# Differential-attention scores as row-split float products: two maps of a head in partitions 0 to 63 and 64 to 127

## The chip, the cores and the metric

The kernel runs on one core of one Trainium2 chip. The metric is the device time of one execution in microseconds (us), lower is better. The time before is the median of three runs.

## The reference, cut to what matters

The reference is a two-layer block over 1024 latent tokens and 256 context tokens, width 1024. Each layer has a combined input projection, three mixers (differential attention with 4 heads, a state-space scan, a Fourier mixer), an output projection and a squared-ReLU MLP. The change touches the attention scores:

```python
def one_block(qblk):                       # 128 queries
    s = jnp.einsum('bqhmd,bkhmd->bmhqk', qblk, k).astype(jnp.float32) * scale
    p = jax.nn.softmax(s, axis=-1)
    w = p[:, 0] - lam * p[:, 1]            # two maps m of each head h
    return jnp.einsum('bhqk,bkhd->bqhd', w.astype(v.dtype), v)
```

A head has two maps, each with its own query and key of 64 elements; the values of a head have 128. Queries of latent tokens see all 1280 keys; in the first layer the context's queries see the 256 context keys.

## The kernel before, in words

Products with float32 accuracy are made of float32r products, a float32r operand taking one pass of TensorE: an operand is split into a high part (its float32r rounding) and a low part (the rest). `stack` (L538 to 546) transposes the normalized queries and keys of a tile of 128 tokens and writes both parts to DRAM: `QD[t, e]` and `KD[h, e]`, e = 0 the high part and e = 1 the low one, with the two maps of a head in rows 0 to 63 and 64 to 127.

`attention` (from L615) runs once per layer, and a *unit* is one head of one tile of 128 queries. Layer 0 has 8 latent tiles and 2 context tiles (32 full units and 8 of context alone), layer 1 has 8 latent tiles (32 full units).

- `load_k` (L620 to 624) loads a head's keys: for each map a tile `ST[h][m]` whose rows 0 to 63 hold the high part and rows 64 to 127 the low part, in four transfers of 64 rows. `load_q` (L626 to 633) loads a tile's queries: `QS[e]` holds part e twice, in the lower and in the upper 64 rows, for both maps. That takes four transfers, and each byte of `QD` is loaded twice. All go through SP's queue.
- `scores` (L635 to 660): a product of 128 rows with `QS[0]` is then high times (high + low), and one with `QS[1]` is low times (high + low). So a map's scores of 512 keys are two products (`product`, L638 to 640). First come the context keys of both maps into `C`, one PSUM bank (four products of 256 columns) with one maximum over both (L647). Then, map by map, the latent keys go into `S`, two banks (four products of 512 columns), with their maximum (L654), the smaller of the negated maxima (L655), and the exponential on ScalarE (L656), which also sums; L657 does the same for `C`.
- `combine` (L662 to 672): one row sum over the other, and map 0 minus lambda times map 1 on VectorE (L668; in layer 1 the last 512 keys on GpSimd, L670 and L671).
- `values` (L674 to 696): ten transposes (L682), copies to SBUF on ScalarE (L683), ten float32 products with the values (L686, two instructions each), the scaling by the row sum (L688).
- The loop at the end takes `combine` and `values` of the unit three before around the `scores` of the new one. `yield` gives three of four units a piece of other work: the state space's gate (`glu`, L1037 to 1050, which reads `HD`) and, in layer 0, the modulation's products (`mod_pe`, L414, 512 columns in float32).

PSUM in this stage has eight banks: pool `s` with two buffers of [128, 1024] (two banks each) and pool `b` with four banks for `C`, the transposes and the value products. A buffer of a pool is given to the next tile when everything that reads the old one is done.

The order of instructions on each engine is fixed when the program is built: a list scheduler takes, of what its own timeline holds ready, what comes first in the program. So instructions of one unit may be put between those of another. `keep_in_program_order(ins)` ties an instruction behind the one traced before it on its engine.

At the start of the stage SP's queue carries, besides queries and keys, the last state-space transfers: `pa_t<-PD` (L945), the stores `HD<-kv_t` (L1017) and the load `kv_t<-HD` (L1037), which L1046 reads.

## Time and profile before

| what | value |
|---|---|
| median of 3 runs | 3081.3 us (3078.29 to 3085.9) |
| the profiled execution's own time | 3084.44 us |
| its span, first to last instruction | 3082.5 us |
| mean granted TensorE clock | 0.983 of full speed |
| busy share: TensorE (PE), weight loads (PEld), VectorE (DVE), ScalarE (ACT), GpSimd (POOL) | 96%, 78%, 64%, 35%, 20% |

A line of the profile names engine, source line and operands; `L640` is a line of the kernel before. The duration of a TensorE product reaches to the modelled end of its result, so consecutive products overlap in the rows: the distance from start to start (*pitch* below) tells what one costs, and the duration of a merged group is (count - 1) pitches and one duration. PEld rows are the weight loads of the products. In the view of busy times by stretch the columns are: stretch (us from the start), its length, busy us of PE, PEld, DVE, ACT and POOL with their counts of instructions (or of the chosen line's engine alone), granted clock, share of the DMA engines, GB/s.

### The profile page before, as it was taken

The page shows a single profiled execution, that of the slowest core. Times are in us where ns is not written, and L with a number is a line of the kernel's source. Part 1 is how long each engine was busy: PE and PEld are TensorE (multiplying, and loading weights), DVE is VectorE, ACT ScalarE, POOL GpSimd, SP SyncE. Part 2 cuts the span into 40 slices and gives each one's busy share as a digit, 9 for nine tenths or more (in the row PEclk, how much of TensorE's full clock was granted, in tenths as well). Part 3 has the DMA queues.
Part 4 walks back from the last instruction along what each step waited for, and adds up shares of the span by engine and source line. Part 5 has one row for each costly group of instructions (what it writes and reads, how often), then busy time and mean ns, then how long its engine had stood idle before and what let it go on. Part 6 is the DMA issues. An engine that isn't in the chain of part 4 may idle for free.

```text
span 3082.5 us, 41061 instructions
## 1 busy us (share of the span) xinstructions
PE 2950.3 (96%) x15309; PEld 2417.6 (78%) x15309; DVE 1972.9 (64%) x3527; ACT 1077.3 (35%) x2387; POOL 620.5 (20%) x534
## 2 busy tenths in 40 slices
PE   5889989999999999999999999989999999999999
PEld 2667767668888888888888777768889888888887
DVE  7786757666577777676545556959866555455444
ACT  5323436656331121121222243437863222211222
POOL 2563420000100000000276123526631000000000
PEclk8999989999999999999999999999999999999999
DMA  7445573435113232231222044571241111111111
GB/s 244 160 150 165 171 172 113 134 110 154 52 49 103 64 98 84 83 95 43 72 74 89 28 148 141 154 182 52 66 139 44 52 45 55 48 48 41 55 48 65
DMA packets 280851, 299.93 MB, mean 97 GB/s; under 512 B 47158, under 2 KB 191948, under 8 KB 280652
## 3 DMA queue, kind: packets, MB, share of 16 engines
q1 hardware_dynamic: 280652, 297.31, 32.1%
q8 instruction: 120, 1.97, 0.3%
q14 instruction: 79, 0.65, 0.1%
HBM read 229.31 MB, written 67.93 MB: 96 GB/s over the span
## 4 chain that ended last, share of the span: by engine, by line
PE 78%; DVE 9%; DMA 5%; ACT 2%; issue 2%; POOL 1%; SPq 0%; DVEq 0%; POOLq 0%; ACTq 0%
PE b_t L1202 26%; PE b_t L1225 25%; PE b_t L1169 6%; PE b_t L575 4%; PE b_t L686 3%; PE s_t L640 3%; PE b_t L414 2%; PE b_t L602 2%; PE b_t L682 1%; DVE mx L654 1%; DMA s_t<-KD 1%; ACT s_t L656 1%; DMA qs_t<-QD 1%; DMA r_t<-in_w_in_dram 1%; DVE w_t L160 1%
## 5 line engine op out<-in xcount | busy, mean ns | idle before, releaser
L1225 PE MATMUL b_t<-hid_t,w_t 128*128 128x512 f32 (+1 forms) x3840 | 809.3, 370 | 0.0
L1202 PE MATMUL b_t<-s_t,w_t 128*128 128x512 f32 (+1 forms) x3840 | 800.4, 369 | 0.0
L1225 PEld LDWEIGHTS b_t<-hid_t,w_t 128*128 128x128 f32 x3840 | 669.9, 189 | 121.3 <-issue 1.4
L1202 PEld LDWEIGHTS b_t<-s_t,w_t 128*128 128x128 f32 x3840 | 669.0, 189 | 121.3 <-issue 1.1
L1227 DVE SCALAR_TENSOR_TENSOR kv_t<-b_t,mod,kv_t 128x512 f32<-128x512 f32 (+1 forms) x640 | 439.8, 695 | 238.6 <-PE b_t L1225 238.0
L159 ACT CAST w_t<-r_t 128x512 fp32r<-128x512 f32 x336 | 195.1, 619 | 796.1 <-PE b_t L1225 528.7
L575 PE MATMUL b_t<-w_t,s_t 128*128 128x512 f32 (+1 forms) x1392 | 357.7, 411 | 10.0 <-DVE kv_t L1227 3.8
L160 DVE TENSOR_TENSOR w_t<-r_t,w_t 128x512 fp32r<-128x512 f32 x320 | 223.7, 726 | 214.1 <-ACT w_t L159 213.5
L575 PEld LDWEIGHTS b_t<-w_t,s_t 128*128 128x128 f32 x1392 | 266.5, 198 | 72.6 <-issue 6.6
L133 POOL TENSOR_TENSOR sm<-sm,mhalf 128x8 f32<-128x8 f32 (+3 forms) x66 | 106.7, 1616 | 543.2 <-DVE sm L693 232.1
L1206 DVE TENSOR_TENSOR t_t<-b_t,t_t 128x512 f32<-128x512 f32 x160 | 101.2, 633 | 139.4 <-ACT t_t L1205 139.3
L881 POOL TENSOR_TENSOR bg_t<-pt_t,bw_t 128x256 f32<-128x256 f32 x56 | 43.8, 782 | 695.4 <-DMA bw_t<-BD 668.7
L686 PE MATMUL b_t<-kv_t,kv_t 128*128 128x128 f32 x1312 | 177.7, 280 | 3.4 <-ACT kv_t L683 3.3
L686 PEld LDWEIGHTS b_t<-kv_t,kv_t 128*128 128x128 f32 x1312 | 163.8, 193 | 16.7 <-ACT kv_t L683 7.2
L654 DVE TENSOR_REDUCE mx<-s_t 128x1 f32<-128x1024 f32 x128 | 155.2, 1219 | 22.5 <-PE s_t L640 21.8
L159 ACT CAST hid_t<-t_t 128x512 fp32r<-128x512 f32 x160 | 92.5, 578 | 207.0 <-DVE t_t L1206 206.9
L1205 ACT ACTIVATE t_t<-b_t 128x512 f32<-128x512 f32 x160 | 88.2, 552 | 207.3 <-PE b_t L1202 207.2
L656 ACT ACTIVATE s_t<-s_t,mx 128x1024 f32<-128x1024 f32 x128 | 143.6, 1122 | 25.1 <-DVE mx L655 19.4
L160 DVE TENSOR_TENSOR hid_t<-t_t,hid_t 128x512 fp32r<-128x512 f32 x160 | 105.8, 662 | 66.2 <-ACT hid_t L159 66.2
L375 DVE SCALAR_TENSOR_TENSOR ac_t<-bg_t,vc,ac_t 128x512 f32<-128x512 f32 x168 | 118.8, 745 | 32.9 <-DMA bg_t<-in_w_mod_dram 32.5
L640 PE MATMUL s_t<-s_t,qs_t 128*128 128x512 f32 x448 | 128.8, 412 | 9.0 <-ACT s_t L656 6.0
L602 PE MATMUL b_t<-w_t,s_t 128*128 128x512 f32 x480 | 116.5, 396 | 2.5 <-DVE w_t L160 1.4
(329 smaller groups left out, 3581.5 us busy)
## 6 DMA issues: line engine op xcount, KB each, us to landing
r_t<-in_w_ff_dram SPq DMA_DIRECT2D x256, 256.0 KB
bg_t<-in_w_mod_dram SPq DMA_DIRECT2D x96, 256.0 KB
r_t<-in_w_in_dram SPq DMA_DIRECT2D x64, 256.0 KB
qs_t<-QD SPq DMA_DIRECT2D x64, 256.0 KB
XD<-kv_t SPq DMA_DIRECT2D x16, 640.0 KB
KD<-t_t SPq DMA_DIRECT2D x40, 256.0 KB
s_t<-KD SPq DMA_DIRECT2D x32, 320.0 KB
QD<-t_t SPq DMA_DIRECT2D x36, 256.0 KB
```

Source lines behind the costliest of these rows:

```text
L159: self.nc.scalar.copy(h, raw)
L160: (eng or self.nc.vector).tensor_tensor(l, raw, h, ALU.subtract)
L575: nc.tensor.matmul(p[:, :cols], a[:, ts], W[k][:, b, :cols], start=(n == 0), stop=(n == 23))
L602: nc.tensor.matmul(p, a[:, ts], W[k][:, b], start=(n == 0), stop=(n == 11))
L640: nc.tensor.matmul(dst, QS[e][:, m, h], ST[h][m][:, a:b], start=(e == 0), stop=(e == 1))
L654: nc.vector.tensor_reduce(mx[:, m, 1:2], S, AX.X, ALU.max, negate=True)
L656: nc.scalar.activation(PR[m][:, 0:SEQ], S, AF.Exp, bias=mx[:, m, 0:1], accum_out=sm[:, m, 1:2])
L686: nc.tensor.matmul(o, WT[:, kt * 128:(kt + 1) * 128], V[kt // 5][:, kt % 5, h * 128:(h + 1) * 128], start=(c == 0), stop=(c == len(ks) - 1))
L1169: nc.tensor.matmul(p[:, :w], W[c][a][:, k], b[k][:, s:s + w], start=(n == 0), stop=(n == 23))
L1202: nc.tensor.matmul(p[:, :w], W[a][:, k], b[k][:, s:s + w], start=(q == 0), stop=(q == 23))
L1225: nc.tensor.matmul(p[:, :w], W[a][:, cs], hid[b][:, s:s + w], start=(q == 0), stop=(q == n - 1))
L1227: nc.vector.scalar_tensor_tensor(xs, p[:, :w], self.mod[l][:, 40 + c, g // 2:g // 2 + 1], xs, ALU.mult, ALU.add)
```

## The change

Each part of `QD` and `KD` is loaded once as it lies in DRAM: both maps of a part in one tile of 128 rows, two transfers instead of four for a tile of queries and for a head's keys. A map's scores are three products over 64 rows (high·high, low·high, high·low) instead of two over 128 rows. Map 0 uses rows 0 to 63 of TensorE and map 1 rows 64 to 127; the products of the two are interleaved by a count of columns and tied in that order. The order for a full unit is, with (map: keys a, product q): C0 q0, S1a q0, C0 q1, S1a q1, C0 q2, S0a q0, S1a q2, S0a q1, S1b q0, S0a q2, S1b q1, S0b q0, S1b q2, S0b q1, S0b q2, then C1 q0 to q2 (a and b are the first and second 512 latent keys). `S` of both maps is one tile of four banks, with one buffer. The maximum of `C` is taken map by map.

```diff
         def load_k(h):
             ST.append([self.s5([128, TOK], F32R) for _ in range(2)])
-            for m in range(2):
-                for e in range(2):
-                    nc.sync.dma_start(ST[h][m][e * 64:e * 64 + 64].bitcast(F32), self.KD[h, e, m * 64:m * 64 + 64])
+            for e in range(2):
+                nc.sync.dma_start(ST[h][e].bitcast(F32), self.KD[h, e])
 
         def load_q(t, pool='qs'):
-            QS = [self.tl(pool, [128, 2, 4, 128], F32R) for _ in range(2)]
+            QS = [self.tl(pool, [128, 4, 128], F32R) for _ in range(2)]
             for e in range(2):
-                src = self.QD[t, e].rearrange('(m d) c -> d m c', m=2)
-                for r in range(2):
-                    dst = QS[e][r * 64:r * 64 + 64].rearrange('p m h c -> p m (h c)')
-                    nc.sync.dma_start(dst.bitcast(F32), src)
+                nc.sync.dma_start(QS[e].bitcast(F32), self.QD[t, e].rearrange('p (h c) -> p h c', h=NH))
             return QS
 
         def scores(h, t, QS, n):
             full = t < 8
-
-            def product(dst, m, a, b):
-                for e in range(2):
-                    nc.tensor.matmul(dst, QS[e][:, m, h], ST[h][m][:, a:b], start=(e == 0), stop=(e == 1))
-
             C = self.pb((128, 2, CTX))
-            for m in range(2):
-                product(C[:, m], m, SEQ, TOK)
+            if full:
+                S = self.tl('s', [128, 2, SEQ])
+                S = [S[:, m] for m in range(2)]
...
-            nc.vector.tensor_reduce(mx[:, :, 0], C, AX.X, ALU.max, negate=True)
             PR = [E[m][n % 4] for m in range(2)]
-            for m in range(2):
-                if full:
-                    S = self.tl('s', [128, SEQ])
-                    for a in (0, 512):
-                        product(S[:, a:a + 512], m, a, a + 512)
-                    nc.vector.tensor_reduce(mx[:, m, 1:2], S, AX.X, ALU.max, negate=True)
-                    nc.vector.tensor_tensor(mx[:, m, 0:1], mx[:, m, 0:1], mx[:, m, 1:2], ALU.min)
-                    nc.scalar.activation(PR[m][:, 0:SEQ], S, AF.Exp, bias=mx[:, m, 0:1], accum_out=sm[:, m, 1:2])
+
+            def product(m, a, q):
+                e, f = ((0, 0), (1, 0), (0, 1))[q]
+                r = slice(m * 64, m * 64 + 64)
+                b = min(a + 512, SEQ) if a < SEQ else TOK
+                dst = S[m][:, a:b] if a < SEQ else C[:, m]
+                return nc.tensor.matmul(dst, QS[e][r, h], ST[h][f][r, a:b], start=(q == 0), stop=(q == 2))
+
+            rows = [[(0, SEQ, q) for q in range(3)], []]
+            if full:
+                rows[0] += [(0, a, q) for a in (0, 512) for q in range(3)]
+                rows[1] += [(1, a, q) for a in (0, 512) for q in range(3)]
+            rows[1] += [(1, SEQ, q) for q in range(3)]
+            at = [0, 0]
+            while rows[0] or rows[1]:
+                m = 0 if rows[0] and (rows[1][0][1] == SEQ or at[0] <= at[1]) else 1
+                x = rows[m].pop(0)
+                at[m] += 288 if x[1] == SEQ else 544
+                ins = product(*x)
+                if full and x[:2] != (1, SEQ) and x != (0, SEQ, 0):
+                    self.tc.keep_in_program_order(ins)
+                if x == (0, SEQ, 2):
+                    nc.vector.tensor_reduce(mx[:, 0, 0:1], C[:, 0], AX.X, ALU.max, negate=True)
+            if full:
+                nc.vector.tensor_reduce(mx[:, 1, 1:2], S[1], AX.X, ALU.max, negate=True)
+            nc.vector.tensor_reduce(mx[:, 1, 0:1], C[:, 1], AX.X, ALU.max, negate=True)
+            for m in ((1, 0) if full else ()):
+                if m == 0:
+                    nc.vector.tensor_reduce(mx[:, m, 1:2], S[m], AX.X, ALU.max, negate=True)
+                nc.vector.tensor_tensor(mx[:, m, 0:1], mx[:, m, 0:1], mx[:, m, 1:2], ALU.min)
+                nc.scalar.activation(PR[m][:, 0:SEQ], S[m], AF.Exp, bias=mx[:, m, 0:1], accum_out=sm[:, m, 1:2])
+            for m in (1, 0):
                 nc.scalar.activation(PR[m][:, SEQ:TOK], C[:, m], AF.Exp, bias=mx[:, m, 0:1], accum_out=sm[:, m, 0:1])
...
-            with self.scope(psum={'s': 2, 'b': 4}, qs=4, ax=3, ot=2, jk=1, bg=1, mw=1):
+            with self.scope(psum={'s': 1, 'b': 4}, qs=4, ax=3, ot=2, jk=1, bg=1, mw=1):
```

## Rows read from the trace of the kernel before

**Rows 1.** Page, part 1: busy us, share of the span, instructions.
```profile
PE 2950.3 (96%) x15309; PEld 2417.6 (78%) x15309; DVE 1972.9 (64%) x3527; ACT 1077.3 (35%) x2387; POOL 620.5 (20%) x534
```

**Rows 2.** Busy times by stretch: the attention of layer 0, then of layer 1.
```profile
440.00:735.00 295.00, 277.87 (x1667) 201.73 (x1668) 203.73 (x407) 193.77 (x516) 19.71 (x18) 1.00 0.41 118
2080.00:2276.00 196.00, 186.21 (x1339) 169.09 (x1338) 167.48 (x326) 159.70 (x422) 126.07 (x78) 0.98 0.22 59
```

**Rows 3.** The same view of L659 alone (DVE, one per full unit).
```profile
446.00:724.00 278.00, 6.16 (x31) 1.00 0.39 116
2100.50:2265.00 164.50, 9.75 (x27) 0.99 0.22 55
```

**Rows 4.** Timeline, PE, layer 0: start, us, engine, line, operation, out<-in, shapes, count.
```profile
450.23 0.63 PE L640 MATMUL b_t<-s_t,w_t 128*128 128x256 f32 x4
...
500.61 1.09 PE L640 MATMUL s_t<-s_t,qs_t 128*128 128x512 f32 x4
501.53 1.25 PE L682 MATMUL b_t<-idn,s_t 128*128 128x128 f32 x10
502.62 1.56 PE L686 MATMUL b_t<-kv_t,kv_t 128*128 128x128 f32 x12
```

**Rows 5.** Timeline, PE, 158 us: products of 64 rows between products of 128.
```profile
157.76 1.09 PE L575 MATMUL b_t<-w_t,s_t 128*128 128x512 f32 x4
158.78 0.27 PE L897 MATMUL f_t<-bg_t,bw_t 64*16 64x112 f32 x1
158.79 0.27 PE L899 MATMUL f_t<-bg_t,bw_t 64*16 64x112 f32 x1
158.89 0.26 PE L897 MATMUL f_t<-bg_t,bw_t 64*16 64x112 f32 x1
...
159.08 1.20 PE L575 MATMUL b_t<-w_t,s_t 128*128 128x512 f32 x4
```

**Rows 6.** Timeline, PEld, 529 us: weight loads of 128 columns.
```profile
529.06 0.57 PEld L421 LDWEIGHTS b_t<-idn,bg_t 2*128 2x128 f32 x8
```

**Rows 7.** Groups of DVE, 2100 to 2265 us: count, busy us, mean ns, idle before.
```profile
L654 DVE TENSOR_REDUCE mx<-s_t 128x1 f32<-128x1024 f32 x54 | 65.8, 1219 | 7.2 <-PE s_t L640 7.1
...
L647 DVE TENSOR_REDUCE mx<-b_t 128x2 f32<-128x512 f32 x26 | 17.9, 687 | 7.1 <-PE b_t L640 6.4
...
L655 DVE TENSOR_TENSOR mx<-mx 128x1 f32<-128x1 f32 x54 | 8.2, 155 | 0.3
```

**Rows 8.** Chain of waits, 2099 us: start, us, an exponential with its sum.
```profile
2099.25 1.21 ACT s_t L656 x2
```

**Rows 9.** Waits of PE, 400 to 735 us: us in total, times, longest.
```profile
PE f_t L970 <- DMA pa_t<-PD: 6.7, 1, 6.7
PE s_t L640 <- ACT s_t L656: 3.1, 10, 0.8
...
PE b_t L1046 <- DMA kv_t<-HD: 2.5, 1, 2.5
```

**Rows 10.** Waits of PE, 2045 to 2276 us.
```profile
PE b_t L1046 <- DMA kv_t<-HD: 7.1, 1, 7.1
PE s_t L640 <- ACT s_t L656: 5.5, 7, 1.4
```

**Rows 11.** Busy times by stretch: start of layer 1's attention; columns as in rows 2.
```profile
2025.00:2045.00 20.00, 20.00 (x100) 16.64 (x99) 13.02 (x29) 4.84 (x14) 8.08 (x6) 1.00 1.04 234
2045.00:2065.00 20.00, 17.66 (x82) 13.79 (x81) 9.90 (x18) 1.08 (x3) 1.22 (x1) 1.00 1.01 221
```

**Rows 12.** Timeline of SP's queue: start, us of issuing, transfers.
```profile
442.32 3.70 SPq L1017 DMA_DIRECT2D HD<-kv_t  x8
...
2048.70 4.69 SPq L632 DMA_DIRECT2D qs_t<-QD  x4
2054.31 8.71 SPq L1017 DMA_DIRECT2D HD<-kv_t  x8
```

**Rows 13.** Page, part 6: transfers by line, KB each.
```profile
qs_t<-QD SPq DMA_DIRECT2D x64, 256.0 KB
```

## The prediction

> **What bounds the kernel now.** The page comes first: PE is busy 96% of the span [rows 1]. The change touches two stretches only, so the busy times by stretch come next: the attention of layer 0 takes 295 us, that of layer 1 196 us, and in the second PE (95%), DVE (85%) and ACT (81%) are all close to full [rows 2]. The reader should see there that a faster PE soon meets DVE and ACT. L659 runs once per full unit and so gives the period: 278 us for 31 units, 8.97 us in layer 0 (other work and context units included), and 164.5 us for 27, 6.09 us in layer 1 [rows 3].
>
> What PE needs for a unit follows from pitches, (duration of a merged row - duration of one) / (count - 1), with one product at 0.39, 0.28, 0.27 and 0.28 us for the four forms: 0.233 us for the 512 columns of L640, 0.117 for its 256 columns, 0.109 for L682 and 0.116 for L686 [rows 4]. A unit's scores are 8 x 0.233 + 4 x 0.117 = 2.33 us, its transposes 10 x 0.109 = 1.09, its value products 20 x 0.116 = 2.32, a quarter of the tile's last four transposes 0.11: 5.85 of layer 1's 6.09 us. PE sets the pace there, with 0.2 us of waiting.
>
> The waits of PE show what else is on the path: 6.7 and 2.5 us for PD and HD in layer 0, 7.1 us for HD in layer 1, and 3.1 and 5.5 us in which scores wait until the exponential has freed `S` [rows 9, 10].
>
> **The scores on PE.** Does 64 + 64 rows run two products at once? The nearest rows say so: L897 (rows 0 to 63) starts at 158.78 and L899 (rows 64 to 127) at 158.79, and the next pair 0.11 later [rows 5]. Each stream then has 6 x 0.233 + 3 x 0.117 = 1.75 us, and the last product of `C` hangs over by 0.12: 1.87 us for 2.33, a gain of 0.46 us.
>
> Going in and out costs some of it. The fourth L575 starts at 157.76 + 3 x 0.233 = 158.46 and the next product was due at 158.69; L897 comes 0.09 later. The way back: a pitch of 0.11 after 158.89 would be 159.00, and L575 comes at 159.08, 0.08 later. The four L575 behind it take 1.20 instead of 1.09 us, so a load that no product covers costs 0.11 [rows 5]; with 128 columns I charge it at the entry too. In and out: 0.09 + 0.11 + 0.08 + 0.11 = 0.39 us. So a unit whose 18 products stand together gains 0.07 us, 64 units 5 us (**-5**). The page TensorEngine Tiling (Array Packing) of the Trainium skill, section Key Properties, says that a change of the tiling mode drains TensorE, which speaks against this change; the trace agrees, 0.09 and 0.08 us late. The page gives no price; without the drain and its bare loads the sum would stand at 64 x 0.46 = 29 us of gain here, with the rows' price it is 5.
>
> Weight loads rise from 12 to 18. Eight loads of 128 columns take 0.57 us, 0.14 of which is one load's own, a pitch of 0.06 [rows 6]: 1.1 us beside 1.87 of products, hidden. The Trainium skill, page TensorE: Matmul & The Clock Gate, section LDWEIGHTS, gives columns / 1.2 as nanoseconds, 107 for one; one after the other, 18 would take 1.92 us, 0.05 over the products, and by that rule the sum would be 3 us longer. The rows' 0.06 stands in the sum.
>
> Two things are not tied. The first product of `C` may be put early, between transposes or value products of another unit; it then costs a second way in and out, 0.39 us, in layer 0, where other work fills PE: 0 to 12 us for 32 units. No row here says how often; every unit would have to be hit for the upper end, so I take a quarter (**+3**). And the eight context units have three products per map, one map after the other with one overlap, 5 x 0.117 for 4 x 0.117, plus 0.39: 8 x 0.5 (**+4**).
>
> **The ring of `S`.** Before, each map had its own buffer. Now both lie in one tile with one buffer, and the next unit's scores wait for both exponentials. From the first product into `S`: bare load 0.11, last product of map 1 at 5 x 0.233, its end 0.39 later: 1.67 us. Then on DVE the maximum of map 1 1.22, of `C` of map 1 about 0.42 (an estimate: L647's 0.69 for 512 columns less half of L654's 1.22 - 0.69), the smaller 0.155, map 0's maximum 1.22 and the smaller 0.155 [rows 7], then map 0's exponential with its sum 1.21 [rows 8]: 6.05 us until `S` is free. Map 1's exponential runs beside map 0's maximum. Before, one map needed 3 x 0.233 + 0.39 + 1.22 + 0.155 + 1.21 = 3.7 of 6.09 us, so the buffers had slack; now there is none, and any work of DVE that gets between is added. DVE has 167.48 / 32 = 5.2 us per unit [rows 2], 1.8 of it outside this chain, with the first `C` maximum 2.2; free for that are 6.05 + 1.67 - 4.84 = 2.9 us from map 0's smaller (at 4.84) to the next unit's first maximum. It fits with little room, so I take 6.15 us for layer 1: 32 x 0.06 (**+2**). Bounds: the ring hidden and PE's 5.78 setting the pace, 32 x -0.31 = -10; half a microsecond of DVE work in the ring of each unit, 6.55, 32 x 0.46 = +15. In layer 0 the mean of 8.97 us hides it; the fourth of the units without other work may lose 0 to 0.5 us, 0 to 4 us (**+1**). `C` now has two maxima, 0.84 for 0.69 us, within the 2.2.
>
> **The transfers.** A tile of queries was four transfers of 256 KB [rows 13], 1.05 MB, and is now half; the keys' bytes stay. From 2025 to 2065 us all DMA engines are full at 221 to 234 GB/s [rows 11], so half a tile is 2.3 us. In layer 1 SP's queue takes 4.7 us to issue tile 1's queries and then 8.7 us for the eight HD stores that took 3.7 in layer 0 [rows 12]: 1.3 MB less ahead of the HD load is 5.7 us, of which the stores can give back 8.7 - 3.7 = 5.0 of PE's 7.1 us wait. In layer 0 half a tile lies ahead of PD (2.3 of 6.7 us), and HD's 2.5 us may go. That is 9.8 us at most and nothing at least, if what the gate needs on ACT or DVE is late next; I take **-7**. Eight key transfers instead of sixteen also shorten SP's queue, counted in these bounds. The exponentials' change of order is free: ACT is 81% busy and they start when DVE lets them.
>
> **Sum.** -5 + 4 + 3 + 2 + 1 - 7 = -2 us against the profiled execution's 3084.4 us (span 3082.5 and 1.9 around it), which lies 3.1 us above the median: 3079 us against 3081.3. 0.3%, 9.2 us, is about what a measurement of this kernel can tell from no change.
>
> **The rivals.** *The ring takes more than it looks (slower).* Place: DVE's order between the two maxima of a unit. Price: layer 1 +15 and layer 0 +4, with the other terms -3 (layer 0's half of the -5) + 4 + 3 - 7: +16, 3097 us. For it: no slack in 6.05, and DVE's idle time before L654 and L647 is only 0.5 us a unit [rows 7]. Against: 2.9 us are open for 2.2. It decides the sign from a period of 6.44 us, where 32 x 0.35 = 11 us outweighs the other terms (-2) by 9.
> *The ring hides and the queues clear (faster).* Layer 1 -10, layer 0 -3 + 4, transfers -10: -19, 3062 us. For it: the 5.5 us of waits for `S` [rows 10] and full DMA engines. Against: the same 6.05.
> *The products don't run side by side*, so that the change doesn't do what it says: 12 x 0.233 + 6 x 0.117 + 0.39 - 2.33 = 1.56 us more in 64 units, 3181 us. The pairs of L897 and L899 speak against it; those have 16 columns of weights and 112 of data in float32, so it is not excluded.
>
> **How the numbers follow.** Forecast 0.42, of which 0.30 lies within 0.3%, 0.10 below and 0.02 above, since its own bounds reach from 3068 to 3092. The slower ring 0.28 (0.26 above, 0.02 within), the faster case 0.26 (0.22 below, 0.04 within), no overlap 0.04. Faster 0.32, same 0.36, slower 0.32. The range reaches to both rings, 3058 to 3104, with some room for the order that the scheduler finds; outside stay the case without overlap and the outer end of either ring, 0.2 together.
>
> **What would show it.** Right: in L640's rows 64-row products of both maps start side by side, and a full unit's 18 take about 1.9 us; layer 1's L659 period is 6.0 to 6.3 us; PE's wait for HD in layer 1 falls to 1 to 4 us. Wrong: PE's waits at L640 for ACT's exponential sum to 15 us or more in layer 1 (the ring), the block's products stand apart in the timeline (extra ways in and out), or their pitch within a map is near 0.47 us (no overlap).

## The result and the profile after

The changed kernel takes 3254.6 us (median of 4 runs, 3252.07 to 3256.13) against 3082.5 for the kernel before (3078.29 to 3085.9, median of 4; the 3081.3 further up was the median of three of them): ratio 1.0557, 95% interval 1.0544 to 1.0571, 172 us slower. 3079 had been predicted.

In code lines the changed kernel stands 6 to 15 lower: L640 is now L646, L647 is L662 (C of map 0) and L665 (C of map 1), L654 is L664 (map 1) and L668 (map 0), L655 is L669, L656 and L657 are L670 and L672, L659 is L674, the combination L665 to L668 is L680 to L683, and L682, L683, L686, L688 are L697, L698, L701, L703. The page's first part, against [rows 1]:

```profile
PE 3029.7 (93%) x15709; PEld 2445.8 (75%) x15709; DVE 2000.1 (61%) x3599; ACT 1089.0 (33%) x2387; POOL 615.3 (19%) x534
```

PE is busy for 79 us more, partly for its 400 more products and partly because products got slower (shown below); the other 93 us it waited. The busy times by stretch, against [rows 2] (columns as there), first the attention of layer 0, then layer 1:

```profile
440.00:794.00 354.00, 306.98 (x1859) 211.83 (x1860) 214.11 (x443) 199.12 (x513) 19.75 (x18) 0.95 0.26 80
2180.00:2420.00 240.00, 189.32 (x1194) 150.55 (x1192) 137.49 (x273) 126.68 (x324) 90.76 (x61) 0.87 0.08 24
```

In layer 1 PE is down to 79% where it stood at 95%, and DVE and ACT are down to 57% and 53%. No engine is full: that is the mark of a chain that goes through several of them. The loss is in both layers: the output projection, which follows the attention, starts its first product at 794.2 us for 734.3 in layer 0 and at 2448.8 for 2276.7 in layer 1, so some 60 of the 172 us are layer 0's. The same view of L674 alone, the L659 of [rows 3]:

```profile
440.00:794.00 354.00, 6.04 (x32) 0.95 0.26 80
2180.00:2420.00 240.00, 5.53 (x24) 0.87 0.08 24
```

24 units in 240 us are a period of 10.0 us; before it was 6.09, and 6.15 was predicted. The groups of DVE, 2180 to 2440 us, against [rows 7], say where it stands; the last row is the same group in layer 0, 440 to 794 us:

```profile
L668 DVE TENSOR_REDUCE mx<-s_t 128x1 f32<-128x1024 f32 x26 | 31.8, 1224 | 35.8 <-ACT s_t L670 35.8
L664 DVE TENSOR_REDUCE mx<-s_t 128x1 f32<-128x1024 f32 x25 | 30.5, 1219 | 6.2 <-PE s_t L646 6.2
...
L674 DVE TENSOR_TENSOR es<-es 128x2 f32<-128x2 f32 x26 | 5.8, 225 | 32.0 <-ACT s_t L672 32.0
...
L668 DVE TENSOR_REDUCE mx<-s_t 128x1 f32<-128x1024 f32 x31 | 37.9, 1224 | 33.3 <-ACT s_t L670 33.1
```

Two waits for ACT, 1.4 and 1.2 us a unit, that the kernel before did not have or hardly had: L668, the maximum of map 0, stands until ACT has done an exponential of `S`, and L674, the sum, until it has done those of `C`. Before, the same sum waited 4.3 us in all for 27 units:

```profile
L659 DVE TENSOR_TENSOR es<-es 128x2 f32<-128x2 f32 x27 | 9.7, 361 | 4.3 <-ACT s_t L657 4.3
```

One unit of the changed kernel in the timeline of PE, DVE, ACT and POOL (start, us; the last two rows are a block 18 us later):

```profile
2252.41 0.38 PE L646 MATMUL b_t<-s_t,qs_t 64*128 64x256 f32 x1
...
2252.90 1.55 PE L646 MATMUL s_t<-s_t,qs_t 64*128 64x512 f32 x11
2253.00 0.16 DVE L674 TENSOR_TENSOR es<-es 128x2 f32<-128x2 f32 x1 [0.65 <-ACT s_t L672]
...
2253.93 1.01 DVE L683 SCALAR_TENSOR_TENSOR s_t<-s_t,rr,s_t 128x768 f32<-128x768 f32 x1
2254.38 0.87 PE L697 MATMUL b_t<-idn,s_t 128*128 128x128 f32 x6
...
2254.86 1.22 DVE L664 TENSOR_REDUCE mx<-s_t 128x1 f32<-128x1024 f32 x1
...
2256.35 1.04 POOL L710 TENSOR_TENSOR ax_t<-ax_t,sm 128x512 f32<-128x512 f32 x1
2256.44 0.96 DVE L669 TENSOR_TENSOR mx<-mx 128x1 f32<-128x1 f32 x1
...
2257.50 1.11 ACT L670 ACTIVATE s_t<-s_t,mx 128x1024 f32<-128x1024 f32 x1 [1.62 <-DVE mx L669]
...
2258.74 1.23 DVE L668 TENSOR_REDUCE mx<-s_t 128x1 f32<-128x1024 f32 x1 [1.33 <-ACT s_t L670]
...
2260.19 1.11 ACT L670 ACTIVATE s_t<-s_t,mx 128x1024 f32<-128x1024 f32 x1 [0.56 <-DVE mx L669]
...
2261.89 0.16 DVE L674 TENSOR_TENSOR es<-es 128x2 f32<-128x2 f32 x1 [0.65 <-ACT s_t L672]
...
2270.67 0.79 PE L646 MATMUL s_t<-s_t,qs_t 64*128 64x512 f32 x1 [1.09 <-ACT s_t L670]
...
2271.26 2.76 PE L646 MATMUL s_t<-s_t,qs_t 64*128 64x512 f32 x11
```

The block itself, 2252.41 to 2254.38 with the way out, takes 1.97 us for nearly all of a unit's scores (2.33 before): the products do run side by side. But behind it everything stands in a row: combination of the unit before (L683), maximum of map 1, exponential of map 1, and only after its end, 2258.61, the maximum of map 0; then its exponential, `C`'s, the sum, and the next combination. From L674 to L674 it is 8.89 us here (10.0 on the mean), with DVE and ACT taking turns. The smaller of the two maxima of map 1, L669, takes 0.96 us here in place of 0.155, beside an operation of POOL; runs 16 to 18 are about that.

What PE waits for, 2045 to 2443 us, against [rows 10]:

```profile
PE b_t L701 <- ACT kv_t L698: 23.7, 18, 2.6
PE s_t L646 <- ACT s_t L670: 18.5, 16, 3.1
PE b_t L697 <- DVE mx L669: 16.1, 11, 2.2
```

Only the second is the ring of `S` that the prediction named; the third reads as DVE's queue, in which older units' work stands behind L668. The wait for HD (7.1 us) is gone from there. In layer 0 (400 to 794 us) PD's 6.7 us are gone, and HD takes as much as both had [rows 9]:

```profile
PE b_t L1061 <- DMA kv_t<-HD: 9.2, 1, 9.2
```

And PE's clock, by the granted clock in the busy times of three short stretches, of which the first and the last hold the two blocks shown above:

```profile
2251.00:2255.00 4.00, 3.99 (x33) 3.22 (x32) 2.48 (x10) 2.67 (x8) 1.43 (x2) 1.00 0.05 15
2256.00:2270.00 14.00, 10.19 (x75) 8.24 (x74) 8.49 (x17) 7.97 (x21) 5.45 (x5) 1.00 0.11 37
2270.00:2274.00 4.00, 3.33 (x15) 2.29 (x15) 1.90 (x5) 1.33 (x5) 2.04 (x1) 0.50 0.01 4
```

After 14 us in which PE was busy for only 10.2, the clock is granted at 0.50, 1.2 GHz, and the same 11 products take 2.76 us for 1.55. So here PE's pauses are paid twice, once as waiting and once in slower products.

### The profile page after: what moved, and what is told of

It reads as the page before. It is cut to its first block, busy times and chain, and to the rows that moved or that the text cites. A ratio compares the mean times of both kernels' runs of the same rounds, so it can differ in the third digit from the quotient of the medians.

```text
span 3254.4 us, 41789 instructions
## 1 busy us (share of the span) xinstructions
PE 3029.7 (93%) x15709; PEld 2445.8 (75%) x15709; DVE 2000.1 (61%) x3599; ACT 1089.0 (33%) x2387; POOL 615.3 (19%) x534
## 4 chain that ended last, share of the span: by engine, by line
PE 73%; DVE 11%; ACT 5%; POOL 2%; DMA 2%; issue 2%; SPq 0%; DVEq 0%; POOLq 0%; ACTq 0%
PE b_t L1217 24%; PE b_t L1240 24%; PE b_t L1184 6%; PE b_t L575 3%; ACT s_t L670 3%; PE s_t L646 3%; PE b_t L602 2%; PE b_t L701 2%; PE b_t L697 2%; PE b_t L414 1%; PE b_t L646 1%; DVE mx L668 1%; DVE s_t L683 1%; PE f_t L1100 1%; DVE mx L664 1%
## 5 line engine op out<-in xcount | busy, mean ns | idle before, releaser
L701 PE MATMUL b_t<-kv_t,kv_t 128*128 128x128 f32 x1312 | 191.1, 290 | 48.6 <-ACT kv_t L698 48.4
L701 PEld LDWEIGHTS b_t<-kv_t,kv_t 128*128 128x128 f32 x1312 | 168.7, 199 | 63.7 <-ACT kv_t L698 57.1
L670 ACT ACTIVATE s_t<-s_t,mx 128x1024 f32<-128x1024 f32 x128 | 142.4, 1112 | 73.1 <-DVE mx L669 72.9
L698 ACT COPY kv_t<-b_t 128x512 f32<-128x512 f32 (+1 forms) x200 | 101.0, 508 | 149.8 <-PE b_t L697 147.5
L646 PE MATMUL s_t<-s_t,qs_t 64*128 64x512 f32 x672 | 133.3, 475 | 18.3 <-ACT s_t L670 18.3
L697 PE MATMUL b_t<-idn,s_t 128*128 128x128 f32 x656 | 114.6, 301 | 37.3 <-DVE mx L669 16.1
```

The costliest lines, as they stand in the source:

```text
L646: return nc.tensor.matmul(dst, QS[e][r, h], ST[h][f][r, a:b], start=(q == 0), stop=(q == 2))
L670: nc.scalar.activation(PR[m][:, 0:SEQ], S[m], AF.Exp, bias=mx[:, m, 0:1], accum_out=sm[:, m, 1:2])
L697: nc.tensor.transpose(p[:, c:c + 128], PR[:, s + c:s + c + 128], self.idn)
L701: nc.tensor.matmul(o, WT[:, kt * 128:(kt + 1) * 128], V[kt // 5][:, kt % 5, h * 128:(h + 1) * 128], start=(c == 0), stop=(c == len(ks) - 1))
```

## The experiments

Ratios are to the kernel before, measured beside each batch of runs (medians of 3084.5 to 3087.4 us), in brackets the 95% interval; diffs are against the changed kernel unless another one is named.

**1. Two tiles for `S`.**

```
-                S = self.tl('s', [128, 2, SEQ])
-                S = [S[:, m] for m in range(2)]
+                S = [self.tl('s', [128, SEQ]) for m in range(2)]
...
-            with self.scope(psum={'s': 1, 'b': 4}, qs=4, ...
+            with self.scope(psum={'s': 2, 'b': 4}, qs=4, ...
```

> The changed kernel with one thing put back: S is two tiles of 1024 columns with a buffer each, as before, in place of one tile with two halves. The 64-row products, their order and their ways in and out stay. Theory (the single tile costs it: map 0's maximum L668 stands behind map 1's exponential L670, 35.8 us of DVE's idle time in 240 us of layer 1, and the next scores behind both exponentials): at least 130 of the 172 us come back, 3080 to 3125 us, L668 waits for PE alone, the period of L674 in layer 1 falls from 10.0 us to 6.0 to 6.8, and the granted clock there returns from 0.86 to about 0.98. Rival (the ways in and out of the 64-row mode cost it, the products of C that stand apart above all): these stay, so at most 40 us come back, 3210 us or more.

3184.2 us, 1.0324 [1.0302, 1.0346]: 70 us come back, between what the two theories said. The wait of map 0's maximum (now L667) for ACT is gone from the groups of DVE, 2130 to 2350 us:

```profile
L667 DVE TENSOR_REDUCE mx<-s_t 128x1 f32<-128x1024 f32 x27 | 32.8, 1215 | 0.0
```

No data goes from that exponential to that maximum; each map has its own banks. With one tile, the second reader is made to wait for the first one on the other engine. The theory that this was nearly all fell: 27 units in these 220 us are still 8.1 us each.

**2. The wait alone.** Map 0's maximum is written ahead of both exponentials; tile and buffer stay.

```
+            if full:
+                nc.vector.tensor_reduce(mx[:, 0, 1:2], S[0], AX.X, ALU.max, negate=True)
             for m in ((1, 0) if full else ()):
-                if m == 0:
-                    nc.vector.tensor_reduce(mx[:, m, 1:2], S[m], AX.X, ALU.max, negate=True)
```

> The changed kernel with one line moved: map 0's maximum of S is written ahead of both exponentials, so that it no longer waits for ACT. S stays one tile with one buffer. If the wait of map 0's maximum for map 1's exponential (and DVE's queue behind it) is what costs, 100 us or more come back, under 3150 us. If the one buffer costs it, the ring is still 1.67 + 1.22 + 0.42 + 1.22 + 0.155 + 1.21 + 1.21 = 7.1 us (three maxima, then two exponentials), no shorter than the 7.3 it has now, and less than 40 us come back, 3215 us or more. If both, between these.

3211.4 us, 1.0408 [1.0388, 1.0428]: 43 back, so the wait and the buffer both cost. In runs 1 and 2 alike the freed maximum also changes DVE's order: both long maxima now stand ahead of `C`'s maximum and of both smaller ones, so map 1's exponential starts later. The 43 us are thus the wait less what this order costs; the separate buffers, with the same order, give the other 27 (run 1 less run 2). The period is still 240 / 28 = 8.6 us, more than the ring of 7.1 that had been worked out, and the sum now waits longer for ACT than in the changed kernel. Waits of DVE, 2180 to 2380 us:

```profile
DVE es L674 <- ACT s_t L672: 61.2, 24, 3.2
```

**3. `C` in tiles of its own**, on top of run 1:

```
-            C = self.pb((128, 2, CTX))
+            C = [self.pb()[:, 0:CTX] for _ in range(2)]
...
-                if full and x[:2] != (1, SEQ) and x != (0, SEQ, 0):
+                if full and x != (0, SEQ, 0):
```

> As the first kernel (two tiles for S), and the two maps' C products write two PSUM tiles of their own in place of the halves of one, so that all 18 products but the first are tied together and C of map 1 need no longer stand apart. If the products of C that stand apart cost what an extra way in and out costs (0.39 us, 64 units, 25 us at most), it is 5 to 25 us faster than the first kernel. If their price is hidden by other waits, it is within 5 us of it; if the two more PSUM buffers per unit (of 4) are missed by the transposes, it is slower than it.

3232.3 us, 1.0482 [1.0463, 1.0501], 48 slower than run 1: the third of the three cases. Waits of PE, 2180 to 2380 us: the transposes stand until ACT has read `C` out of a buffer that they need.

```profile
PE b_t L696 <- ACT s_t L671: 24.8, 16, 2.6
```

**4. The kernel before with one tile for `S`** (diff against it):

```
+            if full:
+                SS = self.tl('s', [128, 2, SEQ])
             for m in range(2):
                 if full:
-                    S = self.tl('s', [128, SEQ])
+                    S = SS[:, m]
...
-            with self.scope(psum={'s': 2, 'b': 4}, qs=4, ...
+            with self.scope(psum={'s': 1, 'b': 4}, qs=4, ...
```

> The kernel before with one thing of the change alone: S is one tile for both maps with one buffer. Products of 128 rows, loads and order of the maps stay as before. Theory (the single tile is the cause): the second map's maximum waits for the first map's exponential, the ring is 0.93 + 0.39 + 1.22 + 0.155 + 1.21 + 1.22 + 0.155 + 1.21 = 6.5 us and more with what stands in DVE's queue, and without any 64-row product it is slower than before by 30 to 170 us, 3110 to 3250 us. Rival (the 64-row products cost it): within 15 us of the kernel before.

3329.1 us, 1.0795 [1.0775, 1.0814]: without one 64-row product the single tile costs 242 us, more than the whole change and more than expected. But part of it is a wait that the changed kernel does not have. Here PE's products of map 1 stand until map 0's exponential, which reads the other half of the tile, is done:

```profile
2214.73 1.11 ACT L658 ACTIVATE s_t<-s_t,mx 128x1024 f32<-128x1024 f32 x1 [0.98 <-DVE mx L657]
...
2215.99 1.19 PE L640 MATMUL s_t<-s_t,w_t 128*128 128x512 f32 x4 [0.55 <-ACT s_t L658]
```

In the changed kernel the products of both maps come ahead of both exponentials. So run 4 shows that a shared tile can cost that much, not what it costs in the change; runs 1 and 2 show that.

**5. The maxima tied** (on top of run 1): each operation marked `keep` follows the one written before it on DVE. The *loop* in the expectation is a chain that closes on itself from unit to unit: a unit's maxima on DVE, its exponentials on ACT, its sum and combination on DVE, and behind these in DVE's queue the next unit's maxima.

```
+            keep = self.tc.keep_in_program_order if full else lambda ins: ins
-            nc.vector.tensor_reduce(mx[:, 1, 0:1], C[:, 1], ...
+            keep(nc.vector.tensor_reduce(mx[:, 1, 0:1], C[:, 1], ...
...
-                    nc.vector.tensor_reduce(mx[:, m, 1:2], S[m], ...
-                nc.vector.tensor_tensor(mx[:, m, 0:1], ...
+                    keep(nc.vector.tensor_reduce(mx[:, m, 1:2], S[m], ...
+                keep(nc.vector.tensor_tensor(mx[:, m, 0:1], ...
```

> Two tiles for S, and DVE's order in a unit tied: maximum of map 1, of its C, the smaller; then maximum of map 0, the smaller (in the first kernel both 1.22 us maxima stood ahead of C's and of both smaller ones). Theory: in layer 1 the pace is a loop through DVE's queue and ACT: maxima, both exponentials of S, both of C, the sum L673 and the combination L679 to L682 of the same unit, which DVE's order puts ahead of the next unit's maxima. In the first kernel 1.22 + 1.22 + 0.41 + 0.36 of maxima, 2 x 1.11 + 0.47 + 0.45 on ACT, 0.16 + 0.17 + 0.22 + 1.02 = 7.7 us and the semaphores, where 7.9 was measured; tied, map 0's maximum runs beside map 1's exponential, 0.9 us less in 32 units of layer 1 and perhaps as much in the quarter of layer 0's that are free: 3140 to 3165 us, period 6.9 to 7.3 us. Rival (the buffers of S, or the products and their ways in and out, set the pace): within 12 us of the first kernel, 3172 us or more.

3159.0 us, 1.0235 [1.0218, 1.0252], 25 back, as the loop says. The loop is not proved by that: a shorter ring of `S` could give the same. In its steady part a unit takes 190 / 26 = 7.3 us, but the waits of DVE there (2110 to 2300 us) hardly name the sum:

```profile
DVE ax_t L703 <- PE b_t L701: 23.7, 24, 1.0
...
DVE es L674 <- ACT s_t L672: 2.5, 2, 1.9
```

One unit's timeline says why. An older unit's scaling (L703) stands ahead of the sum in DVE's queue, and its value product arrives just before `C`'s last exponential ends, at 2170.79:

```profile
2170.55 0.35 DVE L703 TENSOR_SCALAR ax_t<-b_t,rr 128x128 f32<-128x128 f32 x1 [1.00 <-PE b_t L701]
2170.57 0.22 ACT L672 ACTIVATION_READ_ACCUMULATOR s_t<-b_t,mx 128x1 f32 x1
...
2170.82 0.16 DVE L674 TENSOR_TENSOR es<-es 128x2 f32<-128x2 f32 x1
```

So the rows put the wait down to the value product although the sum could not have started earlier; run 13 is the test of that.

**6. The combination two units later** (on top of run 5): it and its sum are tied behind the maxima.

```
-                old = pend.pop(0) if len(pend) > 2 else None
-                if old is not None:
-                    w = combine(*old[:4])
                 pend.append((h, t, *scores(h, t, QS, i * NH + h), AX4, ssq, i * NH + h))
-                if old is not None:
+                if len(pend) > 2:
+                    old = pend.pop(0)
+                    mixed.append((old, combine(*old[:4])))
+                if len(mixed) > 1:
+                    old, w = mixed.pop(0)
                     values(*old[:2], *w, *old[4:])
```

> As the kernel before, and the combination of the two maps (the sum of the exponentials' sums and L679 to L682's operations) is tied behind the next-but-one unit's maxima on DVE, its values following one unit later, so that DVE never waits for the exponentials of the unit that it has just served. Theory (the loop through DVE and ACT is the rest of the loss): period 6.1 to 6.7 us in layer 1, the ring of S or PE setting the pace, 3070 to 3115 us. Rival (PE's ways in and out of the 64-row mode are the rest of the loss): period still over 7 us, 3140 us or more. A mishap that is possible: the fixed order hurts in layer 0, where other work shares DVE; then layer 0 is longer than 340 us and layer 1 short.

3190.3 us, 1.0333 [1.0316, 1.0349]: a miss of both kinds, 31 slower than run 5. PE now waits for POOL's part of the combination, a wait that had not been there; the run decides nothing about the loop.

**7 and 8. What PE alone pays.** The maxima of `S` left out, in run 1's kernel and in the kernel before:

```
-                nc.vector.tensor_reduce(mx[:, 1, 1:2], S[1], AX.X, ALU.max, negate=True)
...
-                nc.vector.tensor_tensor(mx[:, m, 0:1], mx[:, m, 0:1], mx[:, m, 1:2], ALU.min)
+                nc.vector.tensor_scalar(mx[:, m, 0:1], mx[:, m, 0:1], 0.25, None, ALU.mult)
```

> Leaves out the two maxima of S (2 x 1.22 us of DVE a unit); the exponential takes C's maximum alone, at a quarter of the scale so that it stays finite. Two tiles for S. With them gone the loop of DVE and ACT is some 5.2 us and PE sets the pace, so that against its partner (the next kernel, the same left out of the kernel before) it shows what the 64-row products cost on PE alone. The prediction's terms for PE, -5 + 4 + 3, say that the two stand within 10 us of each other. If every unit pays for two ways in and out more (the first product of C, and C of map 1 apart), it is 2 x 0.39 x 64 = 50 us slower than its partner.

> The kernel before without the two maxima of S, the exponential with C's maximum alone at a quarter of the scale: the partner of the kernel before this one. PE sets the pace in both layers: 3060 to 3080 us, the period in layer 1 at PE's 5.8 to 6.0 us. If it were much faster than that, DVE would have set the pace of the kernel before, not PE.

3106.8 us, 1.0067 [1.0052, 1.0082], and 3092.6, 1.0020 [1.0011, 1.0030]; the second is 13 over its range's upper end, 3080. With the maxima out of the way the change costs 14 us, where the prediction's terms for PE add up to 2. Two cautions: run 7 has the new transfers as well, and PE's wait for HD in layer 1 is 1.0 us in it against 6.9 in run 8, so the products alone may cost some 20; and run 8, with work left out, is 7 us slower than the kernel before, as run 14 below is by 9, so a program put in another order moves by that much for a cause that no run shows. The timeline of PE in run 7, one unit:

```profile
2188.51 0.38 PE L645 MATMUL b_t<-s_t,qs_t 64*128 64x256 f32 x1
...
2189.17 1.16 PE L698 MATMUL b_t<-kv_t,kv_t 128*128 128x128 f32 x8
2190.17 0.38 PE L694 MATMUL b_t<-idn,s_t 128*128 128x128 f32 x2
2190.48 1.67 PE L645 MATMUL s_t<-s_t,qs_t 64*128 64x512 f32 x10
2192.08 0.66 PE L694 MATMUL b_t<-idn,s_t 128*128 128x128 f32 x4
2192.66 0.62 PE L645 MATMUL b_t<-s_t,qs_t 64*128 64x256 f32 x3
2193.21 0.66 PE L694 MATMUL b_t<-idn,s_t 128*128 128x128 f32 x4
```

This unit goes into the 64-row mode three times: 0.66 + 1.60 + 0.55 = 2.81 us from first product to the next 128-row one, where the 128-row scores took 2.33. In the whole of layer 1, 32 units, run 7 goes in 75 times and the changed kernel 89 times. Tying products fixes their order and does not keep other work from between them, and the three products of `C` of map 1 are not tied at all. A way in and out is cheaper than charged: the second of the two L694 starts at about 2190.28 (0.38 less one product's 0.27 behind the first), and 2190.48 is 0.20 after it, where 0.11 is the pitch; the last of ten starts at 2190.48 + 1.67 - 0.39 = 2191.76, and 2192.08 is 0.32 after it, where 0.23 would be due. 0.09 each way.

**9. The order alone.** The kernel before, 128-row products, two tiles, with map 1's maximum and exponential and then map 0's behind the products of both, the maxima and the smaller ones tied as in run 5 (diff against it):

```
-            for m in range(2):
-                if full:
-                    S = self.tl('s', [128, SEQ])
+            if full:
+                S = [self.tl('s', [128, SEQ]) for m in range(2)]
+                for m in range(2):
                     for a in (0, 512):
-                        product(S[:, a:a + 512], m, a, a + 512)
+                        product(S[m][:, a:a + 512], m, a, a + 512)
+                nc.vector.tensor_reduce(mx[:, 1, 1:2], S[1], ...
+                for m in (1, 0):
...
```

> The kernel before with its 128-row products, loads and two tiles for S; only the operations behind the products are put in the changed kernel's order: products of both maps first, then map 1's maximum and exponential, then map 0's (in the kernel before, map 0's maximum and exponential run beside map 1's products). Theory (working both maps at once closes a loop through DVE's queue and ACT, whatever the products): maxima and smaller ones 2 x 1.38, the second exponential 1.21, both of C 0.95, sum and combination 1.6, C's maximum 0.69: 7.2 us if nothing lies beside, 6.5 if C's maximum does; layer 1 longer by 32 x 0.4 to 1.1, layer 0 by 0 to 25 us: 3095 to 3145 us. Rival (only the 64-row products and the single tile cost): within 10 us of the kernel before.

3148.6 us, 1.0207 [1.0192, 1.0222], 4 over the range: 64 us lost without the single tile and without a 64-row product. One row of it was not foreseen; run 16 is about that.

**10. One map after the other** (on top of run 1):

```
-                m = 0 if rows[0] and (rows[1][0][1] == SEQ or at[0] <= at[1]) else 1
+                m = 0 if rows[0] else 1
...
+                if x == (0, 512, 2):
+                    nc.vector.tensor_reduce(mx[:, 0, 1:2], S[0], ...
+                    nc.vector.tensor_tensor(mx[:, 0, 0:1], ...
+                    nc.scalar.activation(PR[0][:, 0:SEQ], S[0], ...
```

> Two tiles for S, 64-row products as in the changed kernel, but map 0's nine first and then map 1's nine, with map 0's maximum and exponential written between: no two products run side by side, and the maps are staggered as in the kernel before. PE alone then needs 12 x 0.233 + 6 x 0.117 and a way in and out for 2.33 us: 1.2 to 1.6 us more in 64 units, 75 to 100 us, 3160 to 3190 us, with PE waiting for next to nothing and a period of 7.2 to 7.6 us. That would say that running side by side is real, and that the lockstep of the two maps eats nearly all of it. If the products of the changed kernel don't gain by running side by side, this one, whose loop is shorter, is clearly faster than the order-tied one (3159): 3125 us or less.

3145.0 us, 1.0198 [1.0183, 1.0213]; 27 units in 200 us of layer 1 are 7.4 us each, and PE is full in layer 1 (busy times, columns as in rows 2):

```profile
2120.00:2250.00 130.00, 129.59 (x852) 105.96 (x850) 100.14 (x201) 89.89 (x234) 69.85 (x46) 1.00 0.07 23
```

Better by 15 us than expected, but the reading stands: without two products at once PE needs 7.4 us a unit and sets the pace, and even so this is 14 us faster than run 5, which has them, and level with run 11, the next one. What running side by side gains is lost again by finishing side by side.

**11. All products tied** (on top of run 1, maxima tied as in run 5 with map 0 first), meant to make one whole block: it opens with the map whose buffer comes free last.

```
-            at = [0, 0]
+            at = [1, 0]
...
-                if full and x[:2] != (1, SEQ) and x != (0, SEQ, 0):
+                if full and x != (1, 0, 0):
...
-            for m in ((1, 0) if full else ()):
+            for m in (range(2) if full else ()):
```

> Two tiles for S, maxima tied as in the kernel of 3159 us but map 0 first, and the products tied whole: the block opens with the map whose buffer comes free last, C of map 0 goes beside its next products, C of map 1 is tied at the end. So a unit goes into and out of the 64-row mode mostly once, where the kernel without maxima did so three times (0.66 + 1.60 + 0.55 us a unit, against 1.97 for a whole block). If the loop of DVE and ACT sets layer 1's pace, its period stays at 7.0 to 7.4 us and only layer 0, where PE has other work, gains 0 to 20 us: 3135 to 3162 us. If PE set the pace, both layers gain 0.6 to 0.8 us a unit: 3110 to 3125 us.

3146.9 us, 1.0203 [1.0186, 1.0220]: in the range of the loop, out of that of PE. But the block is not whole. In 28 of layer 1's 32 units it is parted into 5 and 13 products, with six transposes between and a wait for a buffer of `S` ahead of either part:

```profile
2184.28 0.50 PE L645 MATMUL s_t<-s_t,qs_t 64*128 64x512 f32 x1 [0.38 <-ACT s_t L672]
...
2184.94 0.87 PE L699 MATMUL b_t<-idn,s_t 128*128 128x128 f32 x6
2186.43 1.42 PE L645 MATMUL s_t<-s_t,qs_t 64*128 64x512 f32 x9 [0.61 <-ACT s_t L672]
```

PE goes into the 64-row mode 61 times in layer 1, in run 5 64 times. So what a whole block would gain on PE was not tested.

**12. The combination one unit later** (on top of run 11, as in run 6 with `len(pend) > 1`).

> As the kernel before, and the combination of the previous unit is tied behind this unit's maxima on DVE (one unit later; the miss with 3190 us had it two later). The loop is open then, and the ring of S is left: block 1.97, maxima with smaller ones 1.38 + 1.80, exponential 1.2: 6.35 us. Theory: period 6.4 to 6.9 us, 3090 to 3130 us. Rival (a fixed order on DVE makes PE wait for the combination and POOL instead, as in the miss): period over 7.2, 3150 us or more.

3174.6 us, 1.0292 [1.0277, 1.0308]: the rival. Waits of PE, 2110 to 2300 us:

```profile
PE b_t L699 <- POOL s_t L688: 19.0, 11, 2.2
```

**13 and 14. The loop cut.** `C`'s share of the sum left out, in run 5's kernel and in the kernel before:

```
-            if full:
-                nc.vector.tensor_tensor(sm[:, :, 0], sm[:, :, 0], sm[:, :, 1], ALU.add)
...
-            nc.vector.reciprocal(r, sm[:, :, 0])
+            nc.vector.tensor_scalar(r, sm[:, :, 0], 1.0, None, ALU.add)
```

> The kernel of 3159 us (two tiles, maxima tied), and C's share of the sum of exponentials left out: the sum L674 is gone, C's exponentials leave their sums in a tile that nobody reads, and the reciprocal is an addition of 1 of the same shape so that all stays finite. DVE's combination then waits for the exponentials of S alone, and the loop through DVE's queue is shorter by C's two exponentials and the sum, 0.47 + 0.45 + 0.16 = 1.1 us, while the buffers of S, PE's products and all other work stay as they are. If this loop sets the pace of 7.2 us in layer 1, the period falls to 6.2 to 6.7 us (PE at 6.6, the ring of S at 6.35) and the kernel is 20 to 45 us faster: 3114 to 3139 us. If the ring of S or PE sets it, it stays within 10 us of 3159.

> Its partner: the kernel before with the same left out. PE sets the pace there: within 9 us of the kernel before, 3075 to 3094 us. If it is over 15 us faster, DVE's wait for C's exponentials was part of the pace of the kernel before too.

3135.9 us, 1.0170 [1.0155, 1.0185], 23 faster than run 5, and 3093.1, 1.0032 [1.0022, 1.0041], not faster than the kernel before. So the wait for `C`'s exponentials was part of the pace of the one and not of the other. DVE now waits for the exponentials of `S` at the same place (24.1 us, 28 times), and the wait for the value product is gone with the other. The busy times of run 13, 2110 to 2300 us:

```profile
2110.00:2300.00 190.00, 180.37 (x1322) 139.73 (x1323) 140.73 (x280) 141.87 (x362) 109.64 (x66) 1.00 0.09 29
```

PE is back at 95%, from 90% in run 5. The gain is less than the 1.1 us a unit taken out; PE's ways in and out may be next, which no run shows.

**15. One unit more room** (on top of run 12): a fifth buffer of exponentials for each map, the values one unit later.

```
-            PR = [E[m][n % 4] for m in range(2)]
+            PR = [E[m][n % 5] for m in range(2)]
...
-                if len(mixed) > 1:
+                if len(mixed) > 2:
```

> As the kernel of 3175 us (whole block, the previous unit's combination tied behind this unit's maxima), with a fifth buffer of exponentials for each map and the value products one unit later still, so that PE no longer stands waiting for the combination and POOL's 3.6 us (15.4 us of waits in 130 us of layer 1 there). The loop is open and what is left is the ring of S, 6.35 us, and PE. Theory: period 6.4 to 6.8 us in layer 1, 3085 to 3120 us. If the fixed order of DVE alone was what hurt there, it stays at 3150 us or more.

3145.9 us, 1.0201 [1.0184, 1.0218]: 29 faster than run 12, PE's waits for POOL are gone, and yet 26 over the range. Its waits, 2110 to 2300 us, of PE and DVE:

```profile
PE s_t L645 <- ACT s_t L672: 15.6, 23, 3.8
...
DVE mx L663 <- PE s_t L645: 36.8, 27, 3.4
```

PE waits for the exponential to free `S`, DVE waits for PE's block: this is the ring of `S`. With the one chain opened the other holds it at 190 / 27 = 7.0 us, where 6.35 had been summed up with a whole block; here too it stands in two or three pieces in most units. Both chains are longer than PE's need.

**16 to 18. DVE and POOL.** In run 9 the smaller of two maxima (L659), 0.155 us before, took 0.647 on the mean of 57. In run 9's timeline:

```profile
2149.93 1.56 POOL L676 TENSOR_TENSOR s_t<-s_t,s_t 128x512 f32<-128x512 f32 x1
2150.29 1.23 DVE L659 TENSOR_TENSOR mx<-mx 128x1 f32<-128x1 f32 x1
```

The edit, in the kernels of runs 9 and 11 and in the kernel before:

```
-nc.vector.tensor_tensor(mx[:, m, 0:1], mx[:, m, 0:1], mx[:, m, 1:2], ALU.min)
+nc.vector.tensor_scalar(mx[:, m, 0:1], mx[:, m, 0:1], mx[:, m, 1:2], None, ALU.min)
```

> The kernel before with both maps' maxima and exponentials behind the products (3148.6 us), and one operation written otherwise: the smaller of two maxima, an operation of two tensors (L659, 128x1), becomes one of a tensor and a scalar per partition. In that kernel's layer 1, 29 of 64 of them lasted about 1.1 us in place of 0.155, each begun while POOL's product-sum L676 of two tensors ran and ended with it: 29.8 us more in all, of 64 that the kernel lost. If the form with one tensor doesn't wait for POOL, and these 29.8 us lay on the closed loop, it is 18 to 32 us faster: 3116 to 3131 us, and what is left against the kernel before, 30 to 45 us, is the order alone. If the loop only shifts its wait to another place, within 8 us of 3148.6. If the one-tensor form waits for POOL as well, its rows stay at 1.1 us.

> The kernel with the whole block and tied maxima (3147 us), with the smaller written with a scalar per partition as in the run beside it. Only 10 of its 64 in layer 1 stood with POOL, 7.9 us in all: 0 to 10 us faster, 3137 to 3149 us. If it gains over 15 us, the wait for POOL did more than its own length.

> The kernel before with the smaller written with a scalar per partition, the partner of the two beside it: one of 64 stood with POOL there, 0.7 us, so within 6 us of the kernel before, 3077 to 3091 us.

3128.2 us, 1.0140 [1.0125, 1.0155]; 3140.8, 1.0184 [1.0167, 1.0201]; 3083.2, 0.9996 [0.9987, 1.0006]: all three as expected. The groups of DVE of run 16, 2100 to 2300 us, show the operation at 0.21 us:

```profile
L659 DVE TENSOR_SCALAR mx<-mx 128x1 f32<-128x1 f32 x58 | 12.1, 208 | 0.6
```

So 20 of run 9's 64 us were that meeting, and 43 to 44 are the order by itself, with the ties that hold it (3128.2 against 3084.7 beside it); no run has the order without them. In the changed kernel 9 of 64 met in layer 1, 6.4 us, in run 5 11, 9.8 us.

No kernel with the 64-row products came near the kernel before; the best that computes everything is run 17, 1.8% slower.

## Why the prediction was wrong, step by step

**Side by side: right.** 1.87 us were given for the 18 products and 0.39 for the way in and out; a nearly whole block takes 1.97 with its way out. Run 10 shows the same from the other side, 7.4 us a unit with PE full.

**The ring of `S` (+2 us): here it failed**, in a sentence given without a row: "Map 1's exponential runs beside map 0's maximum." It does not, as long as both maps are one tile: map 0's maximum stands until that exponential is done, 1.4 us a unit. Freeing it gives back 43 us of the 172 (run 2, net of the order that comes with it), a buffer for each map another 27 (run 1 less run 2).

**Layer 0 (+1): failed too.** "In layer 0 the mean of 8.97 us hides it", but 60 of the 172 us are lost there. L668 waits 33.1 us for ACT there (27 times), although PE has other work. By the start of the output projection run 1 still loses 40 us in layer 0, run 5 33, and the order alone (run 16) 16.

**The room in DVE's order: the second failure.** The prediction counted 2.2 us of other DVE work and 2.9 us open for it between map 0's smaller and the next maximum, and said "it fits with little room". It counted durations and not when each could start. The sum waits for `C`'s exponentials. By the prediction's own instants: map 0's smaller ends at 4.84, its exponential at 6.05, `C`'s two at about 7.0 (0.47 + 0.45, as the changed kernel has them), and only then come sum and combination, 0.16 + 0.17 + 0.22 + 1.02, up to 8.5; the next maximum stands behind them in DVE's queue, and the first one started at 1.67. That is 6.9 us a unit, over the 6.44 at which the prediction itself put the turning point (that point counts the ring's own +2 twice; without it, it is 6.50). Run 5 (7.3 us with the maxima tied, and a copy of 0.58 us, L698, among the exponentials in ACT's queue) and run 13 (1.1 us out of it, 23 us back) fit that sum. The slower rival named the right place, "DVE's order between the two maxima of a unit", with a price of 19 us that came from half a microsecond and not from this chain.

In the kernel before the chain is open, because the maps are staggered: map 0's maximum and exponential lie beside map 1's products. The change takes that away, and run 16 prices it, 43 us, with old products, separate tiles and tied maxima.

**Order of the maxima.** In the changed kernel it is the one that the prediction had (L664, L665, L669, then L668), because L668 is held up. Only where L668 is freed and nothing ties it do both long maxima go ahead of `C`'s and of both smaller ones; tying them is worth 25 us there (run 5 less run 1). So this is not a loss of the changed kernel, but it hides part of what runs 1 and 2 gave back.

**PE (-5 + 4 + 3): 14 us by runs 7 and 8,** perhaps 20 without the transfers. The ways into the 64-row mode were undercounted (two to three a unit, where the prediction had one and a second in a quarter of layer 0's units; that map 1's products of `C` are not tied either, it left out) and overpriced (0.39; the drains are 0.09 each way, as read from [rows 5], but little of the bare loads shows).

**Transfers (-7): right in layer 1,** where HD's 7.1 us are gone, wrong in layer 0, where HD's wait rose from 2.5 to 9.2 as PD's 6.7 went. Of the 1.3 MB taken off the queue, two halved tiles of queries explain 1.05. Next to 172 it doesn't matter.

**The signs.** Of the signs of being wrong two came: PE's waits at the scores for ACT's exponential reach 18.5 us in layer 1, where 15 was the mark, and `C`'s products stand apart. Of the signs of being right the side-by-side starts, the block's 1.97 us and HD's wait came as well, but not the period: 10.0 us.

**What stays open.** As steps of one path the runs give back 43 (run 2), 27 (run 1) and 25 (run 5), and 73 are left in run 5 (3159.0 against 3085.6 beside it). Of these run 13 takes 23, PE has 14, and the meetings with POOL some 6 to 10 (run 17 gains 6 on run 11 without them). To add them up takes them as independent, which no run shows. Some 25 to 30 us stay open. The ring of `S` (run 15) is a candidate. The lower clock is hardly one: run 5 is granted 0.983 to 0.986 over its whole time, the kernel before beside it 0.984 to 0.987. Nor has any run the new transfers with the old products. The range of 3058 to 3104 was drawn as if the ring could only be one half microsecond longer than its sum; no row said so.

## What to carry to other kernels

Making two streams run side by side also makes them finish side by side: before counting the gain, write down when each follower can start, engine by engine in queue order, around one whole period, and compare that sum with the period, since busy shares say nothing about it. Two halves of one tile read by two engines may be kept in order though no data goes between them; give each consumer its own tile, and look for the wait in the rows. When a price is "it fits", find the one instruction that cannot start earlier, here a sum of 0.16 us.

## What the hardware showed that was not expected

A small operation of two tensors on DVE (L659, 128x1) that begins while POOL's operation of two tensors of 128x512 runs, but for its last 0.06 us, ends only with it: 2150.29 + 1.23 = 2151.52 against 2149.93 + 1.56 = 2151.49 in run 9, 29 times of 64 in that layer (27 beside L676, two beside L700), 29.8 us in all. The form with a scalar per partition was not held up: in run 16 25 of them begin within L676's span and take 0.20 to 0.22 us. The Trainium skill, page SBUF — State Buffer, section Who interferes with whom, says that a DVE instruction with two SBUF inputs contends with a GpSimd instruction that reads SBUF while one with at most one input outside the two-port modes does not; the trace agrees for these two. Beside POOL's operation of one tensor it shows no such wait: in layer 1 of the kernel before, ten of the eleven L655 that begin within L670's span take 0.15 to 0.16 us. The prediction had not looked for it because in the kernel before it happened to 1 of 64.

A kernel whose PE pauses gets slower products as well: 1.55 and 2.76 us for the same 11 products, at a granted 1.00 and 0.50, 18 us apart.
